# Decay rows of Mamba-2 and DeltaNet chunks by broadcast DMA, and five DeltaNet strips ahead of the decays, in a hybrid recurrent layer

## Chip, cores and metric

The kernel runs on one core of a Trainium2 chip. The metric is device time in microseconds of one execution. TensorE (PE) does the matmuls, VectorE (DVE), ScalarE (ACT) and GpSimd (POOL) the rest, and SyncE's queue (SP) issues the DMAs. Each engine runs its instructions in order.

## What is computed

One layer of four parallel head groups on 64 sample tokens (8 sequences of 8) and 1024 prompt tokens: A is RG-LRU, B is Mamba-2 SSD, C is gated DeltaNet, D is S5. Cut to what matters:

```python
z = x @ w_in            # columns: A, A gate, B (x/B/C), B dt, B gate, C (q/k/v), C beta/decay, C gate, D, D gate
A: RG-LRU, width 256, causal conv of width 4
B: causal conv, SiLU, chunked scan with decays exp(cumsum(dt * -exp(a_log)))     # 4 heads
C: causal conv, SiLU, l2norm(q), l2norm(k), chunked WY form with per-head decay  # 4 heads
D: S5 scan, GELU, GLU
mix = concat(A, B, C, D); out = mix @ w_out
x   = layer_norm(ALPHA * x + out)
```

Everything is fp32. In B and C a chunk needs, for each of its four heads, the matrix exp(a[t] - a[s]) for s <= t, where a is the running sum of the log decays within the chunk.

## The kernel before

Work is staged on channels and tokens. `gemm_strip` makes one 128-channel strip of `x @ w_in` for all 1088 tokens. Each fp32 product is split into high and low fp32r parts, so every step of the contraction takes three matmuls (L232 to L234, `pg` of 128x320 or 128x384). For C there are six strips; `early_z` gives their order as 2, 3, 0, 1, 4, 5 (2 and 3 are k, 0 and 1 q, 4 and 5 v).

The generator `s5_run` yields between its stages; the caller runs strips of C between them: one strip after the first stage, two after the second, none after the third. Its last stage holds the GLU matmuls (`glu`, L725 to L727). Then `decays` is called for C and for B (L417 to L445): a softplus of dt in small DVE instructions, four running-sum matmuls into `ac` (L428 to L431), and the tables `ac`, `nac` (its negative), `ea`, `el`, `ed`, each 128 rows by 9 chunks by 4 heads. Its temporaries come from `small`, a pool with five buffers per shape.

`in_c` then goes through C's strips in the same order: the gemm if it hasn't been done, `conv_of` (one ACT tap L266, three DVE taps `acc` L268, then `keep_tail`, a tanh on ACT L279 and the last DVE product `z` L281), and after strips 3 and 1 `norms`: squares on ACT (`sq` L759), column sums on TensorE (`ssq` L762) and an inverse root of small DVE steps (L334 to L343). `keep_tail` copies conv tails into a tile `tails` of the two-buffer pool behind `tmp`.

After that C's chunks (`gdn.prep` and its solve) run merged with `side`, which is the rest: A, B's strips, B's chunks (`ssd.chunk`), gates and the output projection (`pg` L1442 to L1444). There are nine chunks each, chunk 0 for the samples (64 rows) and 1 to 8 for the prompt (128 rows). A chunk of C makes `kh` (DVE L805), `khT` (PE L814), and a triangular inverse in levels: T (L863), then `tb` (DVE L854) and XY (L870, L873), next level; then E, F, J (L884 to L909). A list scheduler in the framework sets the order of the instructions on every engine.

`gammas` (L733 to L745) makes the decay matrix of a chunk: one matmul writes the mask (`negp` for the prompt, `negs` for the samples, L739) into a PSUM bank, four fp32 transposes spread a column of `ac` over 128 columns each and accumulate onto it (L741), and four ACT exponentials with bias `nac` read the bank and write `gam` in SBUF (L744). `prep` calls it with a buffer tag shared with C's other 128x512 tiles, `chunk` with one shared with B's; each has two buffers.

```python
mm(pv, idb[:n, :n], neg.unsqueeze(1).to_broadcast([n, 4, n]), start=True, stop=False)
for j, h in enumerate(heads):
    mm(pv[:, j], ac[:n, ti, h:h + 1].to_broadcast([n, n]), idf[:n, :n], start=False, stop=(j == 3), is_transpose=True)
for j, h in enumerate(heads):
    act(g[:n, j, :n], pv[:, j], AF.Exp, bias=nac[:n, ti, h:h + 1])
```

Of the kernel before, what the change touches and what calls it, by code (L numbers as in the profile page):

```python
# [8 lines left out]
F32 = mybir.dt.float32  # L9
# [4 lines left out]
AF = mybir.ActivationFunctionType  # L14
OP = mybir.AluOpType
# [4 lines left out]
P = 128  # L20
# [32 lines left out]
def hybrid_step(ctx, tc, I, O, dbg=None):  # L53
    nc = tc.nc
    mm = nc.tensor.matmul
    tr = nc.tensor.transpose
    act = nc.scalar.activation
    V = nc.vector
    G = nc.gpsimd
    tt, ts, stt = V.tensor_tensor, V.tensor_scalar, V.scalar_tensor_tensor  # L60
# [12 lines left out]
    dr = ctx.enter_context(tc.tile_pool(name="dr", bufs=1, space=DR))  # L73
# [95 lines left out]
    idf = const([P, P], F32, "idf")  # L169
# [7 lines left out]
    hv = const([P, 20], F32, "hv")  # L177
# [236 lines left out]
            stt(g, g, 1.0, t[:, 4:260], OP.add, OP.mult)  # L414
            nc.sync.dma_start(bg_d[i], g)

    def decays(x, bias, na):  # L417

        xb = small([P, 9, 4], name="xb")
        tt(xb, x, bias.rearrange("p (o h) -> p o h", o=1).to_broadcast([P, 9, 4]), OP.add)  # L420
        d = softplus(xb.rearrange("p a b -> p (a b)"), 36)
        dt = const([P, 9, 4], F32, "dt")
        V.tensor_copy(dt.rearrange("p a b -> p (a b)"), d)
        da = small([P, 9, 4], name="da")
        tt(da, dt, na.rearrange("p (o h) -> p o h", o=1).to_broadcast([P, 9, 4]), OP.mult)
# [12 lines left out]
        ea = const([P, 9, 4], F32, "ea")
        act(ea, ac, AF.Exp)
        el = const([P, 9, 4], F32, "el")  # L440
        act(el.rearrange("p a b -> p (a b)"), ps[:, 40:76], AF.Exp)
        ed = const([P, 9, 4], F32, "ed")
        tt(ed.rearrange("p a b -> p (a b)"), ps[:, 40:76], nacf, OP.add)
        act(ed, ed, AF.Exp)
        return dt, ac, nac, ea, el, ed  # L445

    def chunk_cols(ti):
        return (0, NS) if ti == 0 else (NS + P * (ti - 1), P)
# [281 lines left out]
            nc.sync.dma_start(zd_d[f], s[:, :T])  # L730


    def gammas(wk, ti, ac, nac, heads, ptag, stag, bufs):  # L733

        n = NS if ti == 0 else P
        pr_ = bank("gam", ptag)
        pv = pr_[:n, :4 * n].rearrange("p (h t) -> p h t", h=4)
        neg = negs if ti == 0 else negp
        mm(pv, idb[:n, :n], neg.unsqueeze(1).to_broadcast([n, 4, n]), start=True, stop=False)  # L739
        for j, h in enumerate(heads):  # L740
            mm(pv[:, j], ac[:n, ti, h:h + 1].to_broadcast([n, n]), idf[:n, :n], start=False, stop=(j == 3), is_transpose=True)  # L741
        g = wk.tile([P, 4, P], F32, name=nm("gam"), tag=stag, bufs=bufs)
        for j, h in enumerate(heads):
            act(g[:n, j, :n], pv[:, j], AF.Exp, bias=nac[:n, ti, h:h + 1])  # L744
        return g  # L745

    def h4(z):
# [21 lines left out]
    def gdn(wk, up, q, k, v, rk, rq):  # L769
# [3 lines left out]
        def f16(name, tag, n, bufs):  # L773
            return wk.tile([P, n], F16, name=nm(name), tag=tag, bufs=bufs)

        dt, ac, nac, ea, el, ed = dec_c
        beta = const([P, 9, 4], F32, "beta")
        act(beta, raw[:, :, 4:8], AF.Tanh, scale=0.5)
        ts(beta, beta, 0.5, 0.5, op0=OP.mult, op1=OP.add)
# [14 lines left out]
        def prep(ti):  # L794
# [12 lines left out]
            kd = r1("kd", "vk", 3)  # L807
            for h in range(4):
                act(h4(kd)[:n, h], h4(kh)[:n, h], AF.Copy, scale=ed[:n, ti, h:h + 1])
            gam = gammas(wk, ti, ac, nac, HO, "i", "g", 2)  # L810
            yield 0.6
            pT = bank("khT", "i")
            for hp in range(2):
# [237 lines left out]
    def ssd(wk, up, x, BT, CT):  # L1051
# [3 lines left out]
        def g2(name):  # L1055
            return wk.tile([P, 4, P], F32, name=nm(name), tag="b2", bufs=2)

        dt, ac, nac, ea, el, ed = dec_b
        wd = const([P, 9, 4], F32, "wd")
        tt(wd, ed, dt, OP.mult)  # L1060
        elh = const([P, 9, 2], F32, "elh")
# [7 lines left out]
        def chunk(ti):  # L1069
# [12 lines left out]
            bg = r1("bg")  # L1082
            nc.sync.dma_start(bg[:n], bg_d[ti, :n])
            yield 0.3
            gam = gammas(wk, ti, ac, nac, (0, 1, 2, 3), "b", "b2", 2)
            yield 0.6
            if last:
                yield from finish(*last.pop())
# [461 lines left out]
```

## Time and profile before

| | us |
|---|---|
| median of 3 runs | 604.24 (603.3 to 605.51) |
| the profiled execution, device time | 608.82 |
| its span in the profile | 607.1 |
| busy: TensorE matmuls | 582.5 (96%) |
| busy: TensorE weight loads | 505.9 (83%) |
| busy: VectorE | 461.9 (76%) |
| busy: ScalarE | 320.7 (53%) |
| busy: GpSimd | 57.1 (9%) |
| mean granted TensorE clock | 0.979 of full speed |

Weight loads run beside matmuls. Matmuls are pipelined, so the sum of their busy times counts overlaps; the distance from start to start tells what one costs. The profiled execution is 4.58 us longer than the median of the timed runs, and durations below come from it.

### The profile page before, as it was taken

The page shows a single profiled execution, that of the slowest core. Times are in us where ns is not written, and L with a number is a line of the kernel's source. Part 1 is how long each engine was busy: PE and PEld are TensorE (multiplying, and loading weights), DVE is VectorE, ACT ScalarE, POOL GpSimd, SP SyncE. Part 2 cuts the span into 40 slices and gives each one's busy share as a digit, 9 for nine tenths or more (in the row PEclk, how much of TensorE's full clock was granted, in tenths as well). Part 3 has the DMA queues.
Part 4 walks back from the last instruction along what each step waited for, and adds up shares of the span by engine and source line. Part 5 has one row for each costly group of instructions (what it writes and reads, how often), then busy time and mean ns, then how long its engine had stood idle before and what let it go on. Part 6 is the DMA issues. An engine that isn't in the chain of part 4 may idle for free.

```text
span 607.1 us, 11704 instructions
## 1 busy us (share of the span) xinstructions
PE 582.5 (96%) x4284; PEld 505.9 (83%) x4284; DVE 461.9 (76%) x1372; ACT 320.7 (53%) x877; POOL 57.1 (9%) x165
## 2 busy tenths in 40 slices
PE   5999899998999999999999999999999999999995
PEld 4999899998999886888988888788887876888883
DVE  6997969964548676688887986878796879766655
ACT  5555245345335365979575575767666566222210
POOL 8120000000100010120010010010101001000000
PEclk9999899999789999999999999999999979999998
DMA  8552122041401110001032310100104132221221
GB/s 300 181 157 80 55 64 87 19 125 60 141 18 44 33 37 36 18 19 36 2 101 68 112 32 18 36 28 3 52 1 153 36 124 90 86 105 70 108 101 70
DMA packets 24186, 44.14 MB, mean 73 GB/s; under 512 B 3200, under 2 KB 10432, under 8 KB 24128
## 3 DMA queue, kind: packets, MB, share of 16 engines
q1 hardware_dynamic: 24128, 43.38, 21.8%
q8 instruction: 34, 0.56, 0.4%
q14 instruction: 24, 0.20, 0.1%
HBM read 32.97 MB, written 10.41 MB: 71 GB/s over the span
## 4 chain that ended last, share of the span: by engine, by line
PE 72%; DVE 15%; ACT 5%; issue 3%; DMA 3%; POOL 1%; SPq 1%; DVEq 0%; ACTq 0%; POOLq 0%
PE pg L233 8%; PE pg L232 8%; PE pg L234 8%; PE pg L1443 6%; PE pg L1442 6%; PE pg L1444 6%; PE kq L825 2%; PE ssq L762 1%; DMA wr<-in_w_tiles_dram 1%; DVE acc L268 1%; PE cb L1107 1%; PE pg L405 1%; DVE cm L471 1%; PE pg L406 1%; PE pg L407 1%
## 5 line engine op out<-in xcount | busy, mean ns | idle before, releaser
L232 PE MATMUL pg<-xh,wh 128*128 128x384 f32 (+1 forms) x432 | 149.4, 346 | 0.0
L233 PE MATMUL pg<-xl,wh 128*128 128x384 f32 (+1 forms) x432 | 148.2, 343 | 0.0
L234 PE MATMUL pg<-xh,wl 128*128 128x384 f32 (+1 forms) x432 | 148.0, 343 | 0.0
L232 PEld LDWEIGHTS pg<-xh,wh 128*128 128x128 f32 x432 | 83.1, 192 | 2.7 <-issue 1.3
L234 PEld LDWEIGHTS pg<-xh,wl 128*128 128x128 f32 x432 | 82.8, 192 | 1.7 <-issue 0.8
L233 PEld LDWEIGHTS pg<-xl,wh 128*128 128x128 f32 x432 | 83.0, 192 | 1.1 <-issue 0.3
L1443 PE MATMUL pg<-wol,wh 128*128 128x512 f32 (+1 forms) x144 | 57.6, 402 | 0.0
L1442 PE MATMUL pg<-woh,wh 128*128 128x512 f32 (+1 forms) x144 | 57.6, 401 | 0.0
L1444 PE MATMUL pg<-woh,wl 128*128 128x512 f32 (+1 forms) x144 | 57.6, 401 | 0.0
L268 DVE SCALAR_TENSOR_TENSOR acc<-z,pcol,acc 128x1112 f32<-128x1112 f32 x36 | 49.3, 1372 | 3.3 <-ACT acc L266 3.0
L156 ACT ACTIVATE wh<-wr 128x512 fp32r<-128x512 f32 (+1 forms) x40 | 25.3, 634 | 39.1 <-PE pg L233 32.6
L875 ACT ACTIVATE X<-XY 128x256 f16<-128x256 f32 (+1 forms) x51 | 19.6, 385 | 27.4 <-PE XY L873 27.3
L1444 PEld LDWEIGHTS pg<-woh,wl 128*128 128x128 f32 (+1 forms) x144 | 26.6, 184 | 7.4 <-issue 0.4
L1442 PEld LDWEIGHTS pg<-woh,wh 128*128 128x128 f32 (+1 forms) x144 | 26.5, 184 | 7.4 <-ACT woh L1407 0.4
L1443 PEld LDWEIGHTS pg<-wol,wh 128*128 128x128 f32 (+1 forms) x144 | 26.5, 184 | 7.3 <-issue 0.6
L246 ACT ACTIVATE z<-pg 128x384 f32<-128x384 f32 (+2 forms) x48 | 17.4, 394 | 25.7 <-PE pg L234 24.0
L878 ACT ACTIVATE yb<-XY 64x256 f16<-64x256 f32 x82 | 30.5, 372 | 0.8
L865 DVE TENSOR_TENSOR T<-T,lev 128x256 f16<-128x256 f32 (+1 forms) x51 | 21.5, 421 | 11.4 <-PE T L863 10.2
L157 DVE TENSOR_TENSOR wl<-wr,wh 128x512 fp32r<-128x512 f32 (+1 forms) x40 | 27.8, 694 | 2.0 <-ACT wh L156 1.8
L1445 DVE SCALAR_TENSOR_TENSOR y<-y,pg 128x512 f32<-128x512 f32 (+1 forms) x18 | 12.3, 683 | 15.8 <-PE pg L1444 15.8
L405 PE MATMUL pg<-wh,xh 128*128 128x268 f32 x72 | 21.4, 298 | 2.7 <-ACT bg L410 2.7
L1458 ACT ACTIVATE y<-y,nb,rs 128x1024 f32<-128x1024 f32 (+1 forms) x8 | 10.0, 1244 | 23.9 <-DVE nb L1457 12.8
(444 smaller groups left out, 1334.1 us busy)
## 6 DMA issues: line engine op xcount, KB each, us to landing
wr<-in_w_tiles_dram SPq DMA_DIRECT2D x40, 256.0 KB, 2.8
x<-in_x_t_dram SPq DMA_DIRECT2D x8, 544.0 KB, 4.8
wo<-in_w_out_dram SPq DMA_DIRECT2D x16, 256.0 KB, 3.0
y<-in_x_dram SPq DMA_DIRECT2D x8, 512.0 KB, 3.2
out_y_dram<-y SPq DMA_DIRECT2D x7, 512.0 KB, 2.6
bgd<-bg SPq DMA_DIRECT2D x9, 128.0 KB, 1.7
dud<-us SPq DMA_DIRECT2D x2, 544.0 KB, 4.6
U<-dud SPq DMA_DIRECT2D x16, 68.0 KB, 2.6
```

The costliest lines, as they stand in the source:

```text
L156: act(hv_, wv, AF.Copy)
L157: lo_eng[0].tensor_tensor(lv, wv, hv_.bitcast(F32), OP.subtract)
L232: mm(o, whi[k], xh[:, k, a:b], start=(k == 0), stop=False)
L233: mm(o, whi[k], xl[:, k, a:b], start=False, stop=False)
L234: mm(o, wlo[k], xh[:, k, a:b], start=False, stop=(k == 7))
L268: stt(acc[:, :CL], s[:, j:j + CL], col(wkey, j * nt + i), acc[:, :CL], OP.mult, OP.add)
L405: mm(o, xh[:, k, c0:c0 + P], whi[k], start=(k == 0), stop=False)
L865: tt(t_[:n], pt[:n], lev[:n, l].unsqueeze(1).to_broadcast([n, 4, 64]), OP.mult)
L878: act(yb[s, :, s], pY[s], AF.Copy)
L1442: mm(ps[:n], mh[k_], woh[:, k_, e], start=(k_ == 0), stop=False)
L1443: mm(ps[:n], mh[k_], wol[:, k_, e], start=False, stop=False)
L1444: mm(ps[:n], ml[k_], woh[:, k_, e], start=False, stop=(k_ == 7))
```

## The change

`decays` also sends the running sums to DRAM in transposed form: a copy of `ac` (with the heads in the order in which `gammas` wants them), one PE transpose of 36x128, a copy to SBUF (a `tmp` tile) and a DMA into a scratch of 9 rows of 512 numbers, one scratch for C and one for B. In `gammas` a prompt chunk gets its row broadcast to all 128 partitions by a DMA (256 KB) straight into `gam`; DVE adds the mask in place, and the four exponentials read and write SBUF. The sample chunk stays as it was. The strips of C between S5's stages become one, two, none, two: five strips stand ahead of the decays instead of three.

```diff
+        acT = dr.tile([9, 4 * P], F32, name="act" + key, tag="act" + key)
+        pt = bank("acT")
+        aco = small([P, 36], name="aco")
+        V.tensor_copy(aco.rearrange("p (c a b) -> p c a b", a=2, b=2), ac.rearrange("p c (a b) -> p c b a" if key == "c" else "p c (a b) -> p c a b", a=2))
+        tr(pt[:36, :P], aco, idf)
+        o = tmp("acT")
+        V.tensor_copy(o[:36, :P], pt[:36, :P])
+        nc.sync.dma_start(acT.rearrange("c (h t) -> (c h) t", h=4), o[:36, :P])
+        return dt, ac, nac, ea, el, ed, acT
...
-    def gammas(wk, ti, ac, nac, heads, ptag, stag, bufs):
+    def gammas(wk, ti, ac, nac, acT, heads, ptag, stag, bufs):
 
         n = NS if ti == 0 else P
-        pr_ = bank("gam", ptag)
-        pv = pr_[:n, :4 * n].rearrange("p (h t) -> p h t", h=4)
-        neg = negs if ti == 0 else negp
-        mm(pv, idb[:n, :n], neg.unsqueeze(1).to_broadcast([n, 4, n]), start=True, stop=False)
+        g = wk.tile([P, 4, P], F32, name=nm("gam"), tag=stag, bufs=bufs)
+        if ti:
+            nc.sync.dma_start(g.rearrange("p h t -> p (h t)"), acT[ti:ti + 1].to_broadcast([P, 4 * P]))
+            tt(g, g, negp.unsqueeze(1).to_broadcast([P, 4, P]), OP.add)
+            src = g
+        else:
+            src = bank("gam", ptag)[:n, :4 * n].rearrange("p (h t) -> p h t", h=4)
+            mm(src, idb[:n, :n], negs.unsqueeze(1).to_broadcast([n, 4, n]), start=True, stop=False)
+            for j, h in enumerate(heads):
+                mm(src[:, j], ac[:n, ti, h:h + 1].to_broadcast([n, n]), idf[:n, :n], start=False, stop=(j == 3), is_transpose=True)
         for j, h in enumerate(heads):
-            mm(pv[:, j], ac[:n, ti, h:h + 1].to_broadcast([n, n]), idf[:n, :n], start=False, stop=(j == 3), is_transpose=True)
-        g = wk.tile([P, 4, P], F32, name=nm("gam"), tag=stag, bufs=bufs)
-        for j, h in enumerate(heads):
-            act(g[:n, j, :n], pv[:, j], AF.Exp, bias=nac[:n, ti, h:h + 1])
+            act(g[:n, j, :n], src[:, j], AF.Exp, bias=nac[:n, ti, h:h + 1])
         return g
...
     next(s5_run)
     columns()
-    for i in early_z[:1]:
+    for n in (1, 2, 0):
+        for i in early_z[len(z):len(z) + n]:
+            run(strip_c(i))
+        next(s5_run, None)
+    for i in early_z[len(z):len(z) + 2]:
         run(strip_c(i))
-    next(s5_run)
-    for i in early_z[1:3]:
-        run(strip_c(i))
-    next(s5_run)
     run(s5_run)
```

How the order moves is shown at three places. The first is TensorE from S5's last GLU matmuls to the running sums. Before, the sums of C (`ac_1802`) and of B (`ac_1846`) stand together right behind `glu`:

```order
L725 MATMUL glu_1764<-gh_1716,gh_1708 128x384
L726 MATMUL glu_1764<-gl_1717,gh_1708 128x384
L727 MATMUL glu_1764<-gh_1716,gl_1709 128x384
L428 MATMUL ac_1802<-da_1800,tri_853 128x32
L429 MATMUL ac_1802<-da_1800,tris_867 128x4
L430 MATMUL ac_1802<-da_1800,ones_862 128x32
L431 MATMUL ac_1802<-da_1800,seqm_864 128x4
L428 MATMUL ac_1846<-da_1844,tri_853 128x32
L429 MATMUL ac_1846<-da_1844,tris_867 128x4
L430 MATMUL ac_1846<-da_1844,ones_862 128x32
L431 MATMUL ac_1846<-da_1844,seqm_864 128x4
L232 MATMUL pg_2164<-xh,wh_2101 128x384
```

In the changed kernel B's sums (`ac_2042`), seen here, and B's transpose `acT_2059` stand among gemm matmuls:

```order
L234 MATMUL pg_2259<-xh,wl_2223 128x384
L232 MATMUL pg_2259<-xh,wh_2228 128x384
L428 MATMUL ac_2042<-da_2040,tri_853 128x32
L429 MATMUL ac_2042<-da_2040,tris_867 128x4
L430 MATMUL ac_2042<-da_2040,ones_862 128x32
L431 MATMUL ac_2042<-da_2040,seqm_864 128x4
L233 MATMUL pg_2259<-xl,wh_2228 128x384
L234 MATMUL pg_2259<-xh,wl_2229 128x384
L232 MATMUL pg_2259<-xh,wh_2228 128x384
L233 MATMUL pg_2259<-xl,wh_2228 128x384
L449 MATMUL acT_2059<-idf_89,aco_2060 36x128
L234 MATMUL pg_2259<-xh,wl_2229 128x384
```

From the last output matmul of S5 (`y<-H,lo`) to B's sums there are 96 gemm matmuls in the order before and 181 in the changed one; ahead of `glu` they are 96 and 134. From the program's start to the first `khT` the orders hold 548 and 609 gemm matmuls.

The second place is VectorE at the same point. Before, the last products of the convolutions of strips 3 (`z_1474`) and 0 (`z_1568`) stand ahead of S5's `gl` and of the decays' copies `ac`, and that of strip 2 (`z_1167`) still earlier:

```order
L281 SCALAR_TENSOR_TENSOR z_1474<-z_1474,acc_1875 128x1024
L268 SCALAR_TENSOR_TENSOR acc_1933<-z_1568,pcol_96,acc_1933 128x1112
L157 TENSOR_TENSOR wl_2102<-wr_2099,wh_2101 128x512
L268 SCALAR_TENSOR_TENSOR acc_1933<-z_1568,pcol_96,acc_1933 128x1112
L157 TENSOR_TENSOR wl_2108<-wr_2105,wh_2107 128x512
L280 SCALAR_TENSOR_TENSOR z_1568<-z_1568,acc_1933 128x64
L281 SCALAR_TENSOR_TENSOR z_1568<-z_1568,acc_1933 128x1024
L714 TENSOR_TENSOR gl_1709<-glu_1706,gh_1708 128x512
L714 TENSOR_TENSOR gl_1713<-yt_1295,gh_1712 128x1088
L714 TENSOR_TENSOR gl_1717<-yt_1696,gh_1716 128x1088
L729 SCALAR_TENSOR_TENSOR sg_1720<-sg_1720,yt_1295 128x1088
L434 COPY ac_1807<-ac_1802 128x36
```

In the changed kernel those of strips 2 and 3 follow the decays, behind the copy `acT_2063` and the table `wd`, and taps of the next strips stand between the first steps of the inverse root:

```order
L451 COPY acT_2063<-acT_2059 36x128
L1071 TENSOR_TENSOR wd_4170<-ed_2055,dt_2038 128x36
L281 SCALAR_TENSOR_TENSOR z_1167<-z_1167,acc_2068 128x1024
L281 SCALAR_TENSOR_TENSOR z_1474<-z_1474,acc_2079 128x1024
L268 SCALAR_TENSOR_TENSOR acc_2137<-z_1568,pcol_96,acc_2137 128x1112
L775 TENSOR_SCALAR ssq_2113<-ssq_2090 128x36
L268 SCALAR_TENSOR_TENSOR acc_2137<-z_1568,pcol_96,acc_2137 128x1112
L334 CAST b_2116<-ssq_2113 128x36
L268 SCALAR_TENSOR_TENSOR acc_2148<-z_1774,pcol_96,acc_2148 128x1112
```

So all last products of C's convolutions now stand behind B's decays, and with them the squares and `ssq`.

The third place is TensorE in the inverse of C's last chunk, from T to XY of the last level but one (weight loads of small operands have rows of their own). Before, a matmul of the output `o` of an earlier chunk and seven gemm matmuls stand between T and XY:

```order
L863 MATMUL T_6571<-X_6565,ah 128x64
L863 LDWEIGHTS ah
L863 MATMUL T_6571<-X_6565,ah 128x64
L991 MATMUL o_6700<-W_6497,Pm_5825 128x64
L232 MATMUL pg_6707<-xh,wh_6525 128x384
L233 MATMUL pg_6707<-xl,wh_6525 128x384
L234 MATMUL pg_6707<-xh,wl_6526 128x384
L232 MATMUL pg_6707<-xh,wh_6525 128x384
L233 MATMUL pg_6707<-xl,wh_6525 128x384
L234 MATMUL pg_6707<-xh,wl_6526 128x384
L232 MATMUL pg_6707<-xh,wh_6525 128x384
```

In the changed kernel there are, in the same level, two matmuls of the output projection:

```order
L874 LDWEIGHTS ah
L874 MATMUL T_6523<-X_6517,ah 128x64
L874 LDWEIGHTS ah
L874 MATMUL T_6523<-X_6517,ah 128x64
L874 LDWEIGHTS ah
L874 MATMUL T_6523<-X_6517,ah 128x64
L1454 MATMUL pg_6822<-wol,wh_6753 64x512
L1455 MATMUL pg_6822<-woh,wl_6754 64x512
L881 LDWEIGHTS tb
```

The gemm matmuls that stood here are issued earlier in the changed kernel, and matmuls of the output projection take a part of the places.

## Rows read from the trace of the kernel before

**Rows 1.** The page: busy us (share) xinstructions, then the chain's share by engine.

```profile
PE 582.5 (96%) x4284; PEld 505.9 (83%) x4284; DVE 461.9 (76%) x1372; ACT 320.7 (53%) x877; POOL 57.1 (9%) x165
...
PE 72%; DVE 15%; ACT 5%; issue 3%; DMA 3%; POOL 1%; SPq 1%; DVEq 0%; ACTq 0%; POOLq 0%
```

**Rows 2.** Windows: stretch, its length, busy us by engine, clock, DMA share, GB/s.

```profile
151.80:195.10 43.30, 43.22 (x256) 42.15 (x255) 27.66 (x66) 19.26 (x43) 2.71 (x12) 0.88 0.21 70
196.00:493.00 297.00, 291.05 (x2590) 244.06 (x2589) 235.33 (x662) 195.12 (x587) 27.53 (x69) 1.00 0.14 45
```

**Rows 3.** TensorE's waits: us in total, times, longest.

```profile
PE XY L870 <- DVE tb L854: 2.8, 6, 0.9
...
PE glu L725 <- ACT gh L713: 0.8, 1, 0.8
PE J L906 <- DVE x L902: 0.8, 1, 0.8
PE glu L726 <- DVE gl L714: 0.7, 2, 0.4
```

**Rows 4.** Groups by line and form: busy us, mean ns, idle before.

```profile
L268 DVE SCALAR_TENSOR_TENSOR acc<-z,pcol,acc 128x1112 f32<-128x1112 f32 x36 | 49.3, 1372 | 3.3 <-ACT acc L266 3.0
...
L741 PE MATMUL gam<-idf,ac 128*128 128x128 f32 x64 | 10.6, 278 | 0.0
...
L741 PEld LDWEIGHTS gam<-idf,ac 128*128 128x128 f32 x64 | 7.4, 137 | 0.9
...
L739 PE MATMUL gam<-negp,idb 128*128 128x512 bf16 x16 | 6.2, 386 | 0.0
...
L471 DVE TENSOR_TENSOR cm<-bk 128x512 f32<-128x512 f32 x4 | 2.7, 683 | 0.0
```

**Rows 5.** Timeline of TensorE, a `gammas` call of C: start, us.

```profile
331.74 0.39 PE L739 MATMUL gam<-negp,idb 128*128 128x512 bf16 x1
331.96 0.60 PE L741 MATMUL gam<-idf,ac 128*128 128x128 f32 x4
332.47 0.41 PE L814 MATMUL khT<-idf,kh 128*128 128x128 f32 x2
```

**Rows 6.** DMA issues: count, KB each, us to landing.

```profile
wr<-in_w_tiles_dram SPq DMA_DIRECT2D x40, 256.0 KB, 2.8
...
ln<-in_ln_b_dram SPq DMA_DIRECT2D x1, 512.0 KB, 5.2
```

**Rows 7.** Groups of ScalarE from SBUF and from PSUM.

```profile
L809 ACT ACTIVATE kd<-kh,ed 128x64 f32<-128x64 f32 x32 | 8.5, 338 | 1.1 <-PE w L958 0.9
...
L954 ACT ACTIVATE qd<-ks,ea 128x64 f32<-128x64 f32 x28 | 6.5, 321 | 0.8 <-DVE R L951 0.8
```

**Rows 8.** Timeline of TensorE: `glu` to `ac`, and the first `khT`.

```profile
147.63 0.34 PE L727 MATMUL glu<-gh,gl 128*128 128x384 f32 x1
147.80 0.30 PE L428 MATMUL ac<-da,tri 128*128 128x32 f32 x2
...
195.67 0.34 PE L814 MATMUL khT<-idf,kh 64*128 64x64 f32 x2
```

**Rows 9.** Timeline of VectorE, the inverse roots and the first `kh`.

```profile
156.32 0.19 DVE L764 TENSOR_SCALAR ssq<-ssq 128x36 f32<-128x36 f32 x1 [4.51 <-PE ssq L762]
...
179.69 0.20 DVE L764 TENSOR_SCALAR ssq<-ssq 128x36 f32<-128x36 f32 x1 [4.01 <-PE ssq L762]
...
195.11 0.41 DVE L805 TENSOR_TENSOR kh<-kt,rn 64x256 f32<-64x256 f32 x1
```

**Rows 10.** Timeline of TensorE, a level of C's last chunk, and output matmuls.

```profile
476.28 0.28 PE L863 MATMUL T<-X,ah 128*128 128x64 f16 x4
...
477.57 0.29 PE L870 MATMUL XY<-Y,tb 128*128 128x64 f16 x4
...
506.11 0.39 PE L1443 MATMUL pg<-wol,wh 128*64 128x512 f32 x1
506.34 0.39 PE L1444 MATMUL pg<-woh,wl 128*64 128x512 f32 x1
```

More of the change, by code (lines that the diff above doesn't have):

```diff
@@ L415, in gemm_tok, with decays @@
             nc.sync.dma_start(bg_d[i], g)
-    def decays(x, bias, na):
+    def decays(x, bias, na, key):
         xb = small([P, 9, 4], name="xb")
@@ L444, in decays @@
         act(ed, ed, AF.Exp)
-        return dt, ac, nac, ea, el, ed
+        acT = dr.tile([9, 4 * P], F32, name="act" + key, tag="act" + key)
[7 more added lines that the diff above has]
+        return dt, ac, nac, ea, el, ed, acT
     def chunk_cols(ti):
@@ L774, in f16 @@
             return wk.tile([P, n], F16, name=nm(name), tag=tag, bufs=bufs)
-        dt, ac, nac, ea, el, ed = dec_c
+        dt, ac, nac, ea, el, ed, acT = dec_c
         beta = const([P, 9, 4], F32, "beta")
@@ L809, in prep @@
                 act(h4(kd)[:n, h], h4(kh)[:n, h], AF.Copy, scale=ed[:n, ti, h:h + 1])
-            gam = gammas(wk, ti, ac, nac, HO, "i", "g", 2)
+            gam = gammas(wk, ti, ac, nac, acT, HO, "i", "g", 2)
             yield 0.6
@@ L1056, in g2 @@
             return wk.tile([P, 4, P], F32, name=nm(name), tag="b2", bufs=2)
-        dt, ac, nac, ea, el, ed = dec_b
+        dt, ac, nac, ea, el, ed, acT = dec_b
         wd = const([P, 9, 4], F32, "wd")
@@ L1084, in chunk @@
             yield 0.3
-            gam = gammas(wk, ti, ac, nac, (0, 1, 2, 3), "b", "b2", 2)
+            gam = gammas(wk, ti, ac, nac, acT, (0, 1, 2, 3), "b", "b2", 2)
             yield 0.6
@@ L1293, in hybrid_step @@
     columns()
-    for i in early_z[:1]:
+    for n in (1, 2, 0):
[3 more added lines that the diff above has]
+    for i in early_z[len(z):len(z) + 2]:
         run(strip_c(i))
-    next(s5_run)
-    for i in early_z[1:3]:
-        run(strip_c(i))
-    next(s5_run)
     run(s5_run)
-    dec_c = decays(raw[:, :, 8:12], hv[:, 4:8], nega[:, 4:8])
-    dec_b = decays(raw[:, :, 0:4], hv[:, 0:4], nega[:, 0:4])
+    dec_c = decays(raw[:, :, 8:12], hv[:, 4:8], nega[:, 4:8], "c")
+    dec_b = decays(raw[:, :, 0:4], hv[:, 0:4], nega[:, 0:4], "b")
     dp_.__exit__(None, None, None)
```

## Prediction

> **What bounds the kernel now.** I read the page's busy shares and chain first, then the windows, then TensorE's waits, and only then the single stretches that the change touches. TensorE's matmuls are busy for 582.5 us of the span of 607.1, and PE holds 72% of the chain that ended last, DVE 15%, DMA 3% [rows 1]. The reader should see two things there: TensorE sets the time nearly everywhere, and DVE is the only other engine with a real share of the path. Between 196 and 493 us, where the chunks of B and C run, TensorE is busy for 291.05 of 297 us and DVE for 235.33, which is 79% [rows 2]. The one repeated wait of TensorE for DVE in the chunks is that for `tb`: 2.8 us in six times, the longest 0.9 [rows 3]. Gemms stand in nearly all other gaps. [...]
>
> **What is removed.** Sixteen prompt chunks (eight of B, eight of C) lose one mask matmul and four transposes each. By busy time these are 6.2 + 10.6 = 16.8 us [rows 4]. But matmuls overlap, so I price them from start to start: the mask at 331.74 lets the next start after 0.22 us, the four transposes after 0.51 [rows 5]. 0.73 us times 16 is **11.7 us of TensorE's time removed**. The bounds are 16.8 and the transposes' weight loads alone, 7.4 us [rows 4].
>
> [...] I keep 11.7, because the starts in rows 5 follow each other without a gap.
>
> **What is added on TensorE:** two transposes of the decays, 36x128. Each is one matmul of the removed transposes' kind (278 ns [rows 4]) with its load: 0.6 us for both.
>
> **What is added on DVE:** sixteen adds of 128x512 f32. The nearest row is a product of that shape, 683 ns [rows 4], so 16 x 0.683 = 10.9 us, which takes DVE from 79% to 83% between 196 and 493. Each add waits for a broadcast of 256 KB. The nearest transfers are a weight tile of the same bytes, 2.8 us, and a broadcast of twice the bytes, 5.2 us [rows 6]. Its issue waits on SP until the buffer's last reader is done; what is queued behind it on SP are mostly weight tiles that are due later, so I cost the queue at nothing, and 5.2 us late for a tile if that cover fails. An add costs nothing where gemms stand in the gap. Where TensorE already waits for `tb`, 2.8 us in all [rows 3], I take half as much again: **+1.5 us**. The ends are 0 and 16 waits as long as half the longest in rows 3, 16 x 0.45 = 7.2 us.
>
> **The exponentials** now read SBUF instead of PSUM. ACT's nearest pair is 338 ns from SBUF and 321 from PSUM for 64 columns [rows 7]: 17 ns, and 1.1 us for 64 instructions, on an engine that is half idle (53% busy [rows 1]). I cost it at nothing. [...]
>
> **The moved strips: from S5 to the first chunk of C.** 38 more gemm matmuls stand ahead of `glu`, so the waits there go: 0.8 + 0.7 = 1.5 us [rows 3]. Counted in the order, 609 gemm matmuls are issued at the first `khT` instead of 548. A matmul of 128x384 lets the next start after 0.17 us [rows 8]; one of 128x320 by its width after 0.14. These 61 are then between 8.7 and 10.4, I take 9.9 us of work done early, to be taken off when the two times are compared. By TensorE's work alone `khT` (195.67 before [rows 8]) would come at 195.67 - 1.5 + 0.6 + 9.9 = 204.7, a net of -0.9.
>
> But DVE may not be there. B's small buffers are shared with C's, so its decays run behind C's, and the tile for the convolution tails waits until the transposed decays have been sent. So the last product `z` of strips 2 and 3 and the squares for `ssq` come behind the decays (second pair of fences). B's `ac` stands behind 85 more gemm matmuls than before (first pair): 147.80 + 85 x 0.17 [rows 8] - 1.5 + 1.2 for C's own = 162.0, and copies and transpose take DVE to about 165. From there to the first `kh` DVE has 13 taps of 1.37 us, six products of 1024 columns (1.26 each by the taps' rate), and some 43 smaller ones, about 33 us from start to start [rows 4]. Between 151.8 and 195.1 DVE was idle for 43.3 - 27.66 = 15.6 us [rows 2], 4.51 and 4.01 of it on the two `ssq` [rows 9]. The first is filled by taps now, the second I take as half filled, which leaves 9.1. 165 + 33 + 9.1 = 207.1 for `kh`, and `khT` 0.6 later [rows 8, 9], 207.7: later by 12.0, less 9.9 done early, **+2.0 us**. The ends are -0.9 and, with all 15.6 us of idleness and the work at its busy time (34.8), 216.0 or +10.4. If a slow clock falls into this stretch it is covered, as DVE is later than TensorE.
>
> **The tail.** The work done early is missing later, and the order also lets B and the gates run ahead of C: the last chunk of C stands with little beside it. Before, a level took 1.29 us from T to XY, and six or seven gemm matmuls fill it [rows 10] (third pair of fences). Now there are up to three, mostly output matmuls, which start every 0.23 us [rows 10]. The pair holds two there: 1.29 - 0.12 - 0.46 = 0.71 us idle. Going on in this way through the ten gaps up to the last J (0.69, 1.17, 0.09, 0.71, 0.46, 0.71, 0.23, 0.67, 1.14, 0.36) gives 6.2 us, against 0.8 before, on J [rows 3]: **+5.5 us**. The ends are 0 and ten waits of 0.9, 9.
>
> **Sum:** -11.7 + 2.0 + 5.5 + 1.5 = -2.7 us. The profiled execution took 608.82 with a span of 607.1, which becomes 604.4. It was 4.6 us (0.8%) over the median of the three runs, so I carry the difference to the median: 604.24 - 2.7 = **601.5 us**. A measurement of this kernel can tell about 0.3%, 1.8 us, from no change.
>
> **The rivals.**
> - *The full gain.* The gemms left still fill the last chunk, and DVE reaches `kh` as early as TensorE: -11.7 - 0.9 = -12.6 gives 591.6; with half of the tail's cost 594.4. For it: TensorE is 98% busy in the windows and takes what room it gets. Against it: the third pair of fences. Chance 0.18.
> - *No gain.* Only the loads' room is won: -7.4 + 2.0 + 5.5 = +0.1, 604.3. Or each add costs 0.3 us, 4.8 in place of 1.5: 604.8. For it: DVE at 83% with the adds, and the waits for `tb`. Against it: these waits are 2.8 us in all. Chance 0.24.
> - *Slower, by one wait.* The tile of the tails holds ACT, and with it DVE's products and taps, behind the decays' transfers; DVE keeps its 15.6 us of idleness, and `khT` comes at 216.0: -11.7 + 10.4 + 5.5 + 1.5 = +5.7, 609.9. It decides once the first `khT` is later than 212.1. For it: four convolutions stand in one row. Against it: their taps don't depend on each other and can fill each other's waits. Chance 0.20.
> - My forecast, between 596 and 602.4: 0.38.
>
> **How the numbers follow.** Faster 0.18 + 0.38 = 0.56; within 0.3% 0.24; slower 0.20. The range leaves out the lower half of the full gain and the upper part of the slow case: 594 to 608.
>
> **What would show it.** On TensorE `gam` is left for the samples alone; the adds take 0.68 us; no wait for `glu`; the first `khT` near 208; 5 to 6 us of waits in the last chunk of C; waits for `tb` of about 4 us in the other chunks. I am wrong if broadcasts land later than 5.2 us, if `khT` passes 212, or if the last chunk shows under 2 us of waits.

## The result and the profile after

The changed kernel takes 640.24 us (median of 4 runs, 638.02 to 642.9) against 604.88 us of the kernel before beside it (603.3 to 605.78): a ratio of 1.0573, 95% interval 1.0537 to 1.0609. It is 35 us slower, where 2.7 us faster was forecast. One of the four runs of e15_deadmask below was slow (642.07 us) and is left out of its median.

The page of the changed kernel, with the rows that answer to [rows 1]:

```profile
PE 593.6 (93%) x4206; PEld 514.5 (80%) x4206; DVE 470.8 (74%) x1392; ACT 322.8 (50%) x877; POOL 60.4 (9%) x165
...
PE 70%; DVE 14%; issue 5%; ACT 5%; DMA 3%; POOL 3%; SPq 0%; DVEq 0%; POOLq 0%; ACTq 0%
```

TensorE's matmuls are busy 11 us longer, though 78 of them are gone (4284 before). They are slower, not more: the mean granted clock fell from 0.979 to 0.945. The span grew by 32.9 us, and idle TensorE from 24.6 to 46.4 us. The windows say where. First the kernel before, then the changed one, each cut at its first `khT` and the last J of C (columns as in [rows 2]):

```profile
0.00:195.67 195.67, 184.43 (x1233) 178.33 (x1233) 150.06 (x513) 90.37 (x196) 23.12 (x86) 0.97 0.32 103
195.67:492.95 297.28, 291.33 (x2592) 244.27 (x2591) 235.61 (x662) 195.40 (x588) 27.53 (x69) 1.00 0.14 45
492.95:607.10 114.15, 106.72 (x461) 83.28 (x461) 76.20 (x199) 34.95 (x95) 6.46 (x10) 0.95 0.26 93
```

```profile
0.00:207.25 207.25, 193.72 (x1297) 188.51 (x1297) 150.15 (x513) 94.45 (x205) 25.44 (x86) 0.97 0.31 98
207.25:528.79 321.54, 296.37 (x2464) 244.44 (x2464) 248.91 (x691) 199.04 (x592) 28.46 (x69) 0.93 0.18 58
528.79:640.00 111.21, 103.53 (x447) 81.52 (x447) 71.75 (x190) 29.29 (x82) 6.46 (x10) 0.95 0.25 86
```

The middle window holds C's chunks, with B and the rest beside them. Before, TensorE was idle there for 297.28 - 291.33 = 5.9 us, at a clock of 1.00. After, it is idle for 25.2 us, and the clock averages 0.93, which by estimate loses 321.54 x 0.07 = 22.5 us. The window is 24.3 us longer although 128 fewer matmuls stand in it. The first window is 11.6 us longer, the last 2.9 shorter. In both kernels the work that C's chain doesn't need stands beside it; that the first `khT` comes later was to be made good by work done early, and it wasn't.

TensorE's longest waits in the changed kernel (total, times, longest):

```profile
PE XY L881 <- DVE tb L865: 8.2, 9, 3.4
...
PE T L874 <- ACT X L886: 4.2, 7, 2.2
PE ssq L773 <- ACT sq L770: 3.2, 2, 2.0
PE yT L1157 <- DVE y L1153: 3.1, 5, 1.4
...
PE oT L1027 <- DVE yss L1150: 2.4, 2, 1.6
PE cb L1118 <- DVE M L1110: 2.1, 2, 1.1
```

The wait for `tb` went from 2.8 us [rows 3] to 8.2, and none of the others was over 0.5 us before. The broadcasts themselves behave as forecast: they land after 3.2 us, and DVE's adds waited for them 2.6 us in all (issues of DMAs, then the line of the add):

```profile
gam<-actc SPq DMA_DIRECT2D x8, 256.0 KB, 3.2
gam<-actb SPq DMA_DIRECT2D x8, 256.0 KB, 3.2
```

```profile
L747 DVE TENSOR_TENSOR gam<-gam,negp x16: 673/682/693, 231.8 to 479.9; 128x512 f32<-128x512 f32 x16
...
  DMA gam<-actc: 2.6, 2
```

How a wait becomes more than a wait is seen from 366 to 388 us. First TensorE's timeline, then windows of 2 us there:

```profile
368.17 0.34 PE L234 MATMUL pg<-xh,wl 128*128 128x384 f32 x1
368.96 0.28 PE L874 MATMUL T<-X,ah 128*128 128x64 f16 x4 [0.46 <-ACT X L886]
370.32 0.29 PE L881 MATMUL XY<-Y,tb 128*128 128x64 f16 x4 [1.08 <-DVE tb L865]
370.45 0.28 PE L884 MATMUL XY<-T,yb 128*128 128x64 f16 x4
372.37 0.66 PE L1027 MATMUL oT<-idf,o 128*128 128x128 f32 x2 [1.64 <-DVE yss L1150]
372.82 0.42 PE L874 MATMUL T<-X,ah 128*128 128x64 f16 x4
373.05 0.67 PE L232 MATMUL pg<-xh,wh 128*128 128x384 f32 x1
```

```profile
366.00:368.00 2.00, 2.00 (x21) 1.84 (x20) 1.80 (x5) 1.97 (x9) 0.00 (x0) 1.00 0.00 0
368.00:370.00 2.00, 0.78 (x9) 0.43 (x6) 1.91 (x6) 1.95 (x8) 0.00 (x0) 1.00 0.00 0
370.00:372.00 2.00, 0.41 (x8) 0.29 (x8) 0.79 (x5) 1.99 (x8) 1.02 (x1) 1.00 0.44 135
372.00:374.00 2.00, 1.63 (x9) 1.50 (x10) 1.70 (x8) 1.19 (x4) 0.55 (x1) 0.55 0.19 61
374.00:376.00 2.00, 2.00 (x16) 1.45 (x14) 0.56 (x3) 0.86 (x3) 0.00 (x0) 0.50 0.00 0
...
384.00:386.00 2.00, 2.00 (x8) 1.77 (x6) 1.15 (x4) 0.39 (x1) 0.00 (x0) 0.53 0.00 0
386.00:388.00 2.00, 2.00 (x23) 1.62 (x24) 0.00 (x0) 0.76 (x2) 0.00 (x0) 1.00 0.00 0
```

From 368.17 to 373.05 no gemm matmul starts, and only the levels' own matmuls and a transpose of the outputs (`oT`) stand between the waits: TensorE is busy 0.78 and 0.41 of 2 us. The gemms haven't run out; the next one stands behind `oT` in TensorE's order, and `oT` waits 1.64 us for VectorE. In the next window the granted clock falls to 0.55 and stays at 0.50 up to 384, though TensorE is busy again all the time. At 0.50 the gemm matmuls of 128x384 start every 0.32 us (383.20 to 385.44), at 1.00 every 0.175 (366.44 to 367.49). Here four us with little to do mean some 2.8 us of idle time, and then the low clock takes away nearly seven of the next fourteen, counting each window times 1 - clock. The clock falls to 0.50 in this way near 260, 332, 373, 488 and 519 us in this trace; in the kernel before it doesn't between the first `khT` and the last J, where it averages 1.00.

### The profile page after: what moved, and what is told of

It reads as the page before. It is cut to its first block, busy times and chain, and to the rows that moved or that the text cites. A ratio compares the mean times of both kernels' runs of the same rounds, so it can differ in the third digit from the quotient of the medians.

```text
span 640.0 us, 11581 instructions
## 1 busy us (share of the span) xinstructions
PE 593.6 (93%) x4206; PEld 514.5 (80%) x4206; DVE 470.8 (74%) x1392; ACT 322.8 (50%) x877; POOL 60.4 (9%) x165
## 4 chain that ended last, share of the span: by engine, by line
PE 70%; DVE 14%; issue 5%; ACT 5%; DMA 3%; POOL 3%; SPq 0%; DVEq 0%; POOLq 0%; ACTq 0%
PE pg L232 9%; PE pg L233 9%; PE pg L234 9%; PE pg L1455 5%; PE pg L1454 5%; PE pg L1453 5%; PE ssq L773 2%; DMA wr<-in_w_tiles_dram 2%; POOL ors L1020 1%; PE rg L1225 1%; PE pg L405 1%; PE cb L1118 1%; PE w L969 1%; DVE T L876 1%; PE pg L407 1%
## 5 line engine op out<-in xcount | busy, mean ns | idle before, releaser
L232 PE MATMUL pg<-xh,wh 128*128 128x384 f32 (+1 forms) x432 | 152.5, 353 | 1.1 <-ACT z L246 0.6
L233 PE MATMUL pg<-xl,wh 128*128 128x384 f32 (+1 forms) x432 | 149.9, 347 | 0.0
L232 PEld LDWEIGHTS pg<-xh,wh 128*128 128x128 f32 x432 | 84.8, 196 | 4.1 <-issue 1.4
L233 PEld LDWEIGHTS pg<-xl,wh 128*128 128x128 f32 x432 | 84.8, 196 | 2.9 <-issue 2.0
L234 PEld LDWEIGHTS pg<-xh,wl 128*128 128x128 f32 x432 | 84.3, 195 | 1.2 <-issue 0.3
L246 ACT ACTIVATE z<-pg 128x384 f32<-128x384 f32 (+2 forms) x48 | 17.5, 394 | 44.3 <-PE pg L234 41.6
L876 DVE TENSOR_TENSOR T<-T,lev 128x256 f16<-128x256 f32 (+1 forms) x51 | 21.4, 421 | 15.1 <-PE T L874 14.6
L755 ACT ACTIVATE gam<-gam,nac 128x128 f32<-128x128 f32 (+1 forms) x72 | 23.1, 392 | 4.5 <-DVE gam L747 3.4
L1456 DVE SCALAR_TENSOR_TENSOR y<-y,pg 128x512 f32<-128x512 f32 (+1 forms) x18 | 12.3, 683 | 17.4 <-PE pg L1455 17.4
L881 PEld LDWEIGHTS <-tb 128*128 128x128 f16 (+1 forms) x204 | 9.4, 100 | 18.8 <-DVE tb L865 14.1
```

Source lines behind the costliest of these rows:

```text
L232: mm(o, whi[k], xh[:, k, a:b], start=(k == 0), stop=False)
L233: mm(o, whi[k], xl[:, k, a:b], start=False, stop=False)
L234: mm(o, wlo[k], xh[:, k, a:b], start=False, stop=(k == 7))
L755: act(g[:n, j, :n], src[:, j], AF.Exp, bias=nac[:n, ti, h:h + 1])
L876: tt(t_[:n], pt[:n], lev[:n, l].unsqueeze(1).to_broadcast([n, 4, 64]), OP.mult)
```

## The experiments

The list scheduler orders every kernel anew, so no run differs from another by its edit alone. "Gemms ahead" counts the split gemm matmuls that the order holds before the first `khT`: 764 before, 825 in the change (216 more than the 548 and 609 of the prediction, since an earlier gemm, L405 to L407, is counted too). Idle time and low clock are those of TensorE between the first `khT` and the last J, in the one profiled execution, which can lie some us off the median (635.11 in e14_dead2, 615.21 in e9_bonly). The low clock counts window x (1 - clock); with a clock to two places it is good to about 1.5 us. It is an estimate, which takes TensorE's pace to follow the clock; by the starts of the gemm matmuls above, 0.45 of the time is lost at 0.50. Each ratio is to runs of the kernel before that stood beside that kernel (medians of 604.9 to 605.8 us).

| kernel | median us | ratio to before (95%) | gemms ahead | first khT | idle | low clock |
|---|---|---|---|---|---|---|
| before | 604.88 | 1 | 764 | 195.67 | 5.9 | 0.0 |
| the change | 640.24 | 1.0573 (1.0537 to 1.0609) | 825 | 207.25 | 25.2 | 22.5 |
| e1_strips | 607.28 | 1.0013 (0.9985 to 1.0041) | 750 | 193.27 | 6.4 | 0.0 |
| e2_bcast | 635.64 | 1.0468 (1.0389 to 1.0546) | 752 | 210.58 | 16.1 | 9.3 |
| e3_queue | 642.26 | 1.0588 (1.0535 to 1.0641) | 825 | 206.73 | 26.9 | 19.1 |
| e4_own | 615.99 | 1.0139 (1.0087 to 1.0191) | 750 | 194.51 | 16.6 | 6.1 |
| e8_act | 627.10 | 1.0337 (1.0276 to 1.0397) | 761 | 198.57 | 18.9 | 12.7 |
| e7_addonly | 612.57 | 1.0109 (1.0047 to 1.0171) | 750 | 191.36 | 9.6 | 0.0 |
| e9_bonly | 618.60 | 1.0204 (1.0142 to 1.0266) | 750 | 190.98 | 13.8 | 6.3 |
| e10_conly | 614.32 | 1.0118 (1.0059 to 1.0177) | 749 | 194.23 | 11.4 | 3.1 |
| e11_dead4 | 615.03 | 1.0168 (1.0114 to 1.0222) | 750 | 193.22 | 11.3 | 3.1 |
| e12_deada | 625.54 | 1.0336 (1.0277 to 1.0395) | 825 | 206.87 | 16.8 | 3.0 |
| e6_pooladd | 617.88 | 1.0201 (1.0158 to 1.0243) | 750 | 192.88 | 17.8 | 6.2 |
| e13_noadd | 618.65 | 1.0222 (1.0182 to 1.0261) | 750 | 194.89 | 15.6 | 6.2 |
| e15_deadmask | 627.90 | 1.0362 (1.0344 to 1.0379) | 825 | 206.49 | 20.4 | 6.1 |
| e14_dead2 | 631.35 | 1.0418 (1.0396 to 1.0440) | 825 | 208.17 | 11.5 | 6.1 |

### The two halves, the queue, and the shared buffers

**e1_strips**, the strips alone, in the kernel before:

```diff
+    for n in (1, 2, 0):
+        for i in early_z[len(z):len(z) + n]:
+            run(strip_c(i))
+        next(s5_run, None)
+    for i in early_z[len(z):len(z) + 2]:
+        run(strip_c(i))
```

> Only the strips of C move (1, 2, 0, 2); the decay rows are spread on TensorE as before. In its order 750 gemm matmuls stand ahead of the first khT (764 before, 825 with the whole change; counted with all gemms of the strips). Theory ORDER (the gemms that were pulled ahead leave the chunks without cover; TensorE then idles and its clock falls): 601 to 606, since nothing is pulled ahead. Theory QUEUE (the broadcasts hold the weight tiles behind them on SP): 601 to 606, no broadcasts. Theory ADD (DVE's adds and their latency): 601 to 606. If instead it is over 615, the strips alone carry the loss.

607.28 us, not to be told from before. The waits for `glu` are gone, as forecast, and nothing came of it.

**e2_bcast**, the change with the loop over the strips as before:

```diff
+    for i in early_z[:1]:
+        run(strip_c(i))
+    next(s5_run)
+    for i in early_z[1:3]:
+        run(strip_c(i))
+    next(s5_run)
```

> Only the broadcasts: the decay rows come by DMA, DVE adds the mask; the strips stand as before. 752 gemm matmuls ahead of the first khT. ORDER: within 10 us of before, 595 to 612, since the 61 extra gemms are not pulled ahead. QUEUE: 625 to 640, since the sixteen broadcasts stand on SP as in the whole change. ADD: 630 to 640.

635.64 us. The broadcasts carry nearly the whole loss. TensorE waits before the first chunk (its waits, then the windows around the first `khT`):

```profile
PE glu L733 <- ACT gh L721: 8.8, 1, 8.8
...
PE ssq L773 <- ACT sq L770: 4.0, 1, 4.0
```

```profile
0.00:210.58 210.58, 186.07 (x1224) 179.85 (x1224) 150.20 (x516) 90.96 (x196) 25.13 (x86) 0.93 0.30 96
210.58:519.21 308.63, 292.56 (x2530) 245.15 (x2529) 248.37 (x684) 200.85 (x595) 29.76 (x69) 0.97 0.18 58
```

The first `khT` comes 15 us later than before here, with fewer gemms ahead; TensorE was idle for 210.58 - 186.1 = 24.5 us up to it. ORDER as I had put it (the 61 gemms alone) is therefore not enough; the time lies in the ranges of QUEUE and ADD, which fall below. With the strips moved (the change), gemms fill the idleness ahead of the chunks, and in the chunks TensorE is idle for 25.2 us against 16.1 in e2_bcast. That the gemms issued early are what lacks there is not shown: e12_deada has the same 825 ahead and is idle for 16.8.

**e3_queue**:

```diff
-            nc.sync.dma_start(g.rearrange("p h t -> p (h t)"), acT[ti:ti + 1].to_broadcast([P, 4 * P]))
+            nc.gpsimd.dma_start(g.rearrange("p h t -> p (h t)"), acT[ti:ti + 1].to_broadcast([P, 4 * P]))
```

> The whole change, but the sixteen broadcasts are issued by GpSimd's queue, so that they hold nothing behind them on SP. TensorE's order stays that of the change nearly everywhere (825 gemms ahead of the first khT). ORDER: 630 to 642, nearly the whole loss stays. QUEUE: 600 to 615, the loss goes; ACT's wait of 4.7 us for a weight tile near 218 goes. ADD: 635 to 642.

642.26 us, as the change. QUEUE falls: SP's order is not what costs. ScalarE's wait for a weight tile near 218 us, 4.72 us in the change, is still 3.97 us without any broadcast on SP (ScalarE's timeline of e3_queue):

```profile
217.18 0.63 ACT L156 ACTIVATE wh<-wr 128x512 fp32r<-128x512 f32 x1 [3.97 <-DMA wr<-in_w_tiles_dram]
```

**e4_own**:

```diff
-        aco = small([P, 36], name="aco")
+        aco = const([P, 36], F32, "aco" + key)
...
-        o = tmp("acT")
+        o = const([P, P], F32, "acS" + key)
```

> The whole change, but the two new temporaries of the decays have buffers of their own and share none with the softplus and the conv tails. The order then has 750 gemms ahead of the first khT, and the chunks keep theirs. ORDER: 592 to 605. QUEUE: 625 to 640, the broadcasts stand on SP as in the change. ADD: 630 to 640. The first khT comes near 196 to 200 under all three.

615.99 us: 24 us of the 35 hang on two small buffers. The first `khT` is back at 194.51 (the window from there to the last J):

```profile
194.51:500.95 306.44, 289.88 (x2531) 242.72 (x2531) 250.91 (x695) 200.82 (x595) 29.44 (x69) 0.98 0.18 59
```

QUEUE and ADD as priced fall with it. But ORDER's 592 to 605 wasn't reached either: 11.7 us of TensorE work are gone, and the kernel is still 1.4% slower than before.

**e8_act** gives only the transposed tile its own buffer (the second of e4_own's edits).

> The whole change, but the tile that takes the transposed decays to DRAM has a buffer of its own; only the small copy is still shared with the softplus temporaries. 761 gemms ahead of the first khT (825 with the whole change). Theory TILE (the shared tile makes C's first chunk late and pulls the gemms ahead that later cover the chunks): 614 to 622, first khT at 195 to 199. Theory SMALL (the shared small buffer, B's decays behind C's, does it): 632 to 642, first khT over 203.

627.1 us, between both theories: taken in this order, each of the two shared buffers costs about half, 13 us for the tile (640.24 to 627.10) and 11 for the copy (to 615.99). An own buffer for the copy alone was not run.

### What is left with own buffers

**e7_addonly**, in e1_strips (`zmask` is a tile of zeros):

```diff
+        if ti:
+            tt(g, g, zmask.unsqueeze(1).to_broadcast([P, 4, P]), OP.add)
         return g
```

> The strips moved, the decay rows spread on TensorE as before, and after the exponentials DVE adds a tile of zeros to each prompt chunk's matrix, a 128x512 add as in the change, without any transfer. Theory ADD (sixteen adds more on DVE delay the chunks): 613 to 620 (607 plus most of 11 us of DVE's time, TensorE's work not reduced). Theory LANDING (the broadcast that waits for its buffer, 3.2 us, is what costs): 606 to 609.

612.57 us, just under ADD's range and well over LANDING's: the adds alone, with TensorE's work kept, cost 5.3 us over e1_strips, half of DVE's 11 us, and the clock stays up:

```profile
191.36:497.39 306.03, 296.46 (x2607) 247.41 (x2606) 248.22 (x687) 197.30 (x593) 28.26 (x69) 1.00 0.13 44
```

**e9_bonly** and **e10_conly** keep the broadcast for one of the two (`"b"`; `"c"` in the other), the old matmuls for the other:

```diff
+        if key != "b":
+            return dt, ac, nac, ea, el, ed, None
...
-        if ti:
+        if ti and acT is not None:
```

> Own buffers, the strips moved, and the broadcast for B's chunks alone; C's matrices are made on TensorE as before. Theory CHAIN (C's chunks follow each other and set the end, so that only what lies in C's chain costs): 600 to 607, B's eight chunks cost nothing. Theory EVEN (each add costs the same wherever it stands): 609 to 612, half of what both cost together (615.99 against 607.28).

> Own buffers, the strips moved, and the broadcast for C's chunks alone; B's matrices are made on TensorE as before. CHAIN: 612 to 618, nearly all of what both cost together. EVEN: 609 to 612.

618.6 and 614.32 us. C's alone lies in CHAIN's range, but B's alone doesn't, so both CHAIN and EVEN fall: B's broadcasts alone cost as much as both together, and so do C's. In e9_bonly the clock falls most in one stretch like that above (windows of 2 us):

```profile
376.00:378.00 2.00, 0.60 (x12) 0.36 (x11) 1.93 (x8) 1.95 (x7) 0.00 (x0) 1.00 0.00 0
...
382.00:384.00 2.00, 2.00 (x15) 1.62 (x14) 1.47 (x3) 1.07 (x4) 0.00 (x0) 0.50 0.00 0
```

Why B's alone is no better stays open; its order differs from e4_own's in all later chunks.

**e6_pooladd**, in e4_own:

```diff
-            tt(g, g, negp.unsqueeze(1).to_broadcast([P, 4, P]), OP.add)
+            G.tensor_tensor(g, g, negp.unsqueeze(1).to_broadcast([P, 4, P]), OP.add)
```

> Own buffers as in e4_own, with the mask added by GpSimd instead of DVE. If DVE's adds are what lengthens the chunks (e7_addonly cost 5 us over e1_strips): 605 to 612. If it is the way from buffer to transfer to add to exponential, or the missing TensorE work: 614 to 625, since GpSimd's add is no faster.

617.88 us. The add takes 1163 ns there instead of 682, and with DVE freed of it the kernel is no faster than e4_own; the slower add may hide a gain, which the next run excludes:

```profile
L747 POOL TENSOR_TENSOR gam<-gam,negp x16: 1157/1163/1663, 214.2 to 460.3; 128x512 f32<-128x512 f32 x16
```

**e13_noadd**, in e4_own:

```diff
-            tt(g, g, negp.unsqueeze(1).to_broadcast([P, 4, P]), OP.add)
...
-            act(g[:n, j, :n], src[:, j], AF.Exp, bias=nac[:n, ti, h:h + 1])
+            act(g[:n, j, :n], src[:, j], AF.Exp, bias=(ac if ti else nac)[:n, ti, h:h + 1])
```

> Own buffers as in e4_own with the broadcasts, but without the sixteen adds of the mask, and with the exponentials' bias of the other sign so that they stay finite: the mask is left out of the decay matrices of the prompt chunks. ADD (the add in the way from buffer to exponential is what the chunks lose): 600 to 608. COVER with the transfers (the missing TensorE work and the way over the DMA): 610 to 618, as e4_own.

618.65 us (this kernel leaves the mask out of its result). Where TensorE's work has been taken away, taking the adds away gains nothing. ADD falls as the cause of e4_own's loss.

### Useless work put back

**e11_dead4** (in e4_own) and **e12_deada** (in the change):

```diff
             src = g
+            dead = bank("gam", ptag)[:n, :4 * n].rearrange("p (h t) -> p h t", h=4)
+            mm(dead, idb[:n, :n], negp.unsqueeze(1).to_broadcast([n, 4, n]), start=True, stop=False)
+            for j, h in enumerate(heads):
+                mm(dead[:, j], ac[:n, ti, h:h + 1].to_broadcast([n, n]), idf[:n, :n], start=False, stop=(j == 3), is_transpose=True)
```

> Own buffers as in e4_own, the broadcasts and DVE's adds, and beside them the mask matmul and four transposes of every prompt chunk are still done on TensorE, their result read by nobody: the 11.7 us of TensorE work that the change removes are put back. Theory COVER (from the first khT to the last J the chunks of C follow each other at the pace of their own waits; work taken off TensorE returns as idle time, and the clock falls behind it): no slower than e4_own by more than 3 us, 608 to 619, with fewer us lost to a low clock between first khT and last J than the 6.1 of e4_own. Theory THROUGHPUT (TensorE's work sets the time): 625 to 629, all of the 11.7 us on top.

> The whole change with the same unread matmuls put back. COVER: 628 to 643, within 3 us of the change or faster, with less than the 22.5 us that the change loses to a low clock between first khT and last J. THROUGHPUT: 650 to 654.

615.03 us against e4_own's 615.99, and 625.54 against the change's 640.24. 11.7 us of matmuls that nobody reads cost nothing in the one and make the other **14.7 us faster**, below COVER's range of 628 to 643. Between first `khT` and last J (e11_dead4, then e12_deada):

```profile
193.22:500.76 307.54, 296.23 (x2606) 248.31 (x2605) 247.38 (x690) 197.78 (x589) 26.94 (x69) 0.99 0.19 57
```

```profile
206.87:510.42 303.55, 286.77 (x2535) 235.67 (x2534) 246.22 (x685) 196.40 (x585) 29.60 (x69) 0.99 0.19 59
```

**e15_deadmask** puts back the mask matmul alone, **e14_dead2** everything twice.

> The whole change with only the mask matmul of every prompt chunk put back, unread: about 0.22 us each, 3.5 us of TensorE work in all, a third of the work that the change removes. COVER (idle TensorE in the chunks and the low clock behind it are the loss, each bit of work put back fills some): between e12_deada and the change, 628 to 638. ORDER LUCK (e12_deada was a better order by accident, work put back as such changes nothing or costs): 640 to 646.

> The whole change with the unread mask matmuls and transposes put in twice, 23.4 us of TensorE work, double what the change removes. COVER: the first 11.7 us filled idle time, the second meets chunks with less left to fill, so 624 to 634, still faster than the change. THROUGHPUT: 660 to 666. ORDER LUCK: 640 to 655.

627.90 and 631.35 us, the first at the lower edge of COVER's range, the second in it. With 0, 3.5, 11.7 and 23.4 us of unread work the change takes 640.2, 627.9, 625.5 and 631.4 us. THROUGHPUT, +11.7 us or more, falls, and so does ORDER LUCK as I had priced it. What the low clock loses in the chunks goes from 22.5 us to 6.1, 3.0 and 6.1 with it (e15_deadmask, then e14_dead2):

```profile
206.49:511.10 304.61, 284.18 (x2469) 233.10 (x2468) 245.45 (x683) 195.62 (x583) 27.69 (x69) 0.98 0.19 58
```

```profile
208.17:514.21 306.04, 294.57 (x2592) 244.53 (x2591) 241.76 (x670) 192.75 (x571) 27.57 (x68) 0.98 0.17 55
```

What these runs don't separate is the work itself from the order that it brings: with unread matmuls in the list the scheduler also spreads the gemms otherwise. From about 228 us on TensorE's order differs between the change and e12_deada. A bad order in the change, which any added matmul breaks up, is a rival that stands, and two readings speak for it. The least work put back, 3.5 us, already brings 12.3 of the 14.7 us: idle time falls from 25.2 to 20.4 us, but the low clock's loss from 22.5 to 6.1. And in e12_deada, in the level of the same chunk at which the change stands idle from 370.5 to 372.4, no unread matmul stands between T and XY, but gemms in another order, on both sides of `oT`:

```profile
366.48 0.28 PE L878 MATMUL T<-X,ah 128*128 128x64 f16 x4
366.59 0.42 PE L234 MATMUL pg<-xh,wl 128*128 128x384 f32 x1
366.85 0.33 PE L232 MATMUL pg<-xh,wh 128*128 128x384 f32 x1
368.00 0.44 PE L1031 MATMUL oT<-idf,o 128*128 128x128 f32 x2 [0.83 <-DVE o L1028]
...
368.83 0.29 PE L885 MATMUL XY<-Y,tb 128*128 128x64 f16 x4
```

That chunk's levels take as long there, 17.7 us from the first T to the last (353.21 to 370.88), as in the change, 17.4 (355.42 to 372.82). The difference comes behind them: to the next chunk's first T it is 16.4 us in e12_deada and 24.0 in the change, at the low clock. So in this chunk the chain keeps its pace whether TensorE has other work or not, and the time goes with the low clock behind it. Whether the missing work or the order brought the low clock about stays open.

Put in a row, the medians make up the loss: strips 605.6 to 607.3 (within noise), DVE's adds +5.3 (e7_addonly), the transfers and the decays' own steps +2.5 (e11_dead4), the two shared buffers +10.5 (e12_deada), TensorE's work taken away +14.7 (the change). These shares hold for this row alone: with the work taken away first, that step costs 1.0 us (e11_dead4 to e4_own) and the shared buffers 24.3 (e4_own to the change). No kernel was faster than the one before.

## Why the prediction was wrong, point by point

**What is removed: the step that failed.** I took 11.7 us of TensorE's time as gained because the starts in [rows 5] follow each other without a gap. The work is indeed gone. But a gain of the span it is only if TensorE's throughput sets the pace, and in the chunks the waits of C's levels do wherever the order puts no other work beside them. Instead of a gain of 11.7 us the runs show none (e4_own is 1.0 us slower than e11_dead4), or a loss of 14.7 (the change against e12_deada). In the prediction's own terms, the window from the first `khT` to the last J was to become 14.6 us shorter, with all the early work taken out of it (-11.7 - 9.9 + 5.5 + 1.5), and became 24.3 longer: TensorE's work at full clock fell by 17.5 us where 21.6 were booked, idle time grew by 19.3 where 7.0 were booked, and the low clock took 22.5 where nothing was. The failure is therefore in the waits and the clock that came with the removed work more than in the size of that work.

The lower bound, 7.4 us by the transposes' weight loads alone [rows 4], which *No gain* takes, would still have been a gain, and the runs show none.

**"9.9 us of work done early, to be taken off": failed likewise.** The first `khT` was forecast at 207.7 and came at 207.25:

```profile
207.25 0.34 PE L825 MATMUL khT<-idf,kh 64*128 64x64 f32 x2
```

The walk over DVE's work came out to half a us, and e4_own and e8_act bear out its shared buffers (first `khT` at 194.51 and 198.57). That it is so close is partly luck: DVE was through with the decays at 162.5 where 165 was forecast, then idle for 13.0 us up to `kh` where 9.1 was, and busy for 30.9 where 33 was. Nor was the slow clock covered there: DVE's longest wait, 5.29 us for `ssq`, ends at 173.66, and TensorE's granted clock is 0.50 from 168 to 174. But of the 61 matmuls done early nothing came back: the window from `khT` to J grew by 24.3 us instead of shrinking. Both of these steps are one error, counted twice: work taken from beside a chain of waits was booked as time.

**Added on DVE.** The adds take 682 ns, the landing 3.2 us, the wait for landings 2.6 us in all: the rows were read rightly. The cost, +1.5 us forecast, is 5.3 us with TensorE's work kept (e7_addonly) and not measurable with TensorE's work gone (e13_noadd). The waits for `tb` were forecast at about 4 us outside the last chunk; they are 6.8 there and 8.2 in all. They were not the only repeated wait of TensorE for DVE before, either: `yT` waited for `y` twice, 0.4 us in all, and 3.1 us in five times after.

**The tail.** Waits in the last chunk were forecast at 5 to 6 us; after the last `khT` of C at 497 they are 3.1 us, beside a granted clock of 0.82 that takes another 5.7:

```profile
497.42:529.25 31.83, 28.36 (x213) 21.25 (x214) 24.24 (x78) 18.22 (x53) 2.52 (x4) 0.82 0.28 85
```

The idleness I looked for mainly at the end stands in all chunks: 19.3 us more than before where 5.5 + 1.5 were forecast.

**The clock: no term at all.** 22.5 us were lost to the low clock between first `khT` and last J, by the estimate of the table, where the kernel before lost none. I had priced each wait at its own length, and said of the clock only that it would be covered ahead of the first `khT`. It is the largest term of the result.

**The rivals.** The slower one had the right wait, the tile of the tails, with the chance of 0.20. Its point of decision, a `khT` later than 212.1, wasn't reached, and the kernel was slower all the same, since its sum held the same two gains. No rival came past 609.9 us, 30 us short: all priced the waits at their own length and none had the clock. Two small slips change nothing: 12.0 less 9.9 is 2.1 and 6.2 less 0.8 is 5.4, which cancel in the sum, and *No gain* leaves out the +1.5 us of the adds, with which it comes to 605.8.

**The exponentials from SBUF** and SP's queue were costed at nothing; e3_queue bears out the queue, and no run tried the exponentials alone. The trace gives their size: the 64 of 128 columns take 403 ns each instead of 373, 2.6 us more in all where 1.1 was estimated.

## What to carry to other kernels

Where a chain of waits runs beside filler work, work removed from the engine that runs both is not yet a gain (11.7 us here, and e4_own is 1.0 us slower than e11_dead4): ask first what will stand in the gaps of the chain afterwards, and whether the order puts it there. A small temporary put into a shared pool can cost more than the edit saves: 24 us here for some 1.3 KB a partition (10.5 with the unread matmuls in). A cheap test of such a case is to put the removed work back unread: if the time doesn't rise (615.03 us here, against 615.99), that work didn't set it. Where a scheduler makes the order anew, lay both orders side by side before calling the work itself the cause.

## What had not been expected of the hardware

With useless matmuls in it a kernel ran faster, 625.54 us instead of 640.24. The trace shows what came between: after 4 us in which TensorE was busy for 1.19, the granted clock stood at 0.50 for ten us while TensorE was busy without a break. There 2.8 us of idle time and the low clock behind it come to between 9 and 10 us of TensorE's time. No fixed price follows from that. In the same trace TensorE waits 3.40 us for `tb` up to 259.45, and the clock, 0.50 from 260 to 262, is back at 1.00 from 263 on; a wait of 1.37 us that ends at 485.91 has 15 us at 0.50 behind it (two waits of the timeline, then two windows):

```profile
259.45 0.32 PE L881 MATMUL XY<-Y,tb 128*128 128x64 f16 x4 [3.40 <-DVE tb L865]
...
485.91 0.44 PE L1157 MATMUL yT<-idf,y 128*128 128x128 f32 x2 [1.37 <-DVE y L1153]
```

```profile
263.00:264.00 1.00, 1.00 (x14) 0.83 (x13) 0.34 (x3) 0.26 (x1) 0.50 (x1) 1.00 0.00 0
...
490.00:505.00 15.00, 15.00 (x74) 12.68 (x73) 6.32 (x26) 3.49 (x12) 0.85 (x2) 0.50 0.14 49
```

From the change to e12_deada the median fell by 14.7 us, the idle time between first `khT` and last J from 25.2 us to 16.8, and what the low clock loses there from 22.5 to 3.0.
